# Turns for the rotating halves and a written order for VectorE in a dense expert pass

## The chip, the cores and the metric

The kernel runs on one core of one Trainium2 chip. The metric is the device time of one execution in microseconds; the kernel before takes 3657.54 us (median of three runs, 3656.35 to 3660.28). The engines are named as the profile names them: PE (TensorE, matrix products into PSUM), DVE (VectorE), ACT (ScalarE), POOL (GpSimd, which issues the gathers here) and SP (SyncE, which issues the other DMAs).

## The reference

One layer of a diffusion backbone for 9 tiles of 128 tokens (1 of context, 8 of latents): adaptive norm, one wide projection, a gated MLP over chunks, a bidirectional recurrent scan, a merge, and then PEER, a retrieval over 128 x 128 = 16384 single-neuron experts. The change lies in PEER, whose core is this:

```python
v1, i1 = lax.top_k(s[:, :, 0], PEER_TOPK)          # 8 heads, 16 of 128 keys, two halves
v2, i2 = lax.top_k(s[:, :, 1], PEER_TOPK)
cand = v1[..., :, None] + v2[..., None, :]         # 256 candidates a head
top_v, top_j = lax.top_k(cand, PEER_TOPK)          # 16 of them: expert numbers idx, gates g
...
ue = jnp.take(u_tab, ib, axis=0)                   # 128 experts a token
ve = jnp.take(v_tab, ib, axis=0)
a = jax.nn.gelu(jnp.einsum('bd,bed->be', xb, ue)) * gb
return jnp.einsum('be,bed->bd', a, ve)
```

Everything is in fp32 (the large products as three products of split halves).

## The kernel before

PEER is done in two ways. Four of the nine token tiles (GATHER) fetch the rows of their chosen experts: for each of 128 chosen experts of a token, POOL gathers a row of `u_tab` (tile `gu`), DVE takes its dot product with the token (`jk`, one instruction a row), after 16 rows ACT applies gelu (`act`), DVE multiplies by the gates, and then 16 rows of `v_tab` (`gv`) are added into `acc`, one DVE instruction each. A gathered tile has 256 such rows. The other five tiles (DENSE, 640 tokens) compute all 16384 experts with a gate matrix that is nearly empty: this is the dense pass, 128 expert tiles e of 128 experts.

For an expert tile, `hidden` makes 48 matmuls (two halves of 320 tokens, eight pieces of depth, three products of split halves) into PSUM tiles `pH`, ACT applies gelu into `a`, DVE multiplies by the gates `Gt`, and `a` is split into `aH` (ACT) and `aL` (DVE). Two 512 KB tables are loaded by SP and split in the same way: u (for the expert tile after) and v. The output product of three token tiles (`out_res`, 18 matmuls an expert tile) stays in six PSUM banks `pout` over the whole pass. For the other two token tiles there is no bank left: `out_rot` makes, after every GI = 4 expert tiles, four groups of 12 matmuls (two token tiles, two halves of 512 columns, the products of four expert tiles), each into a PSUM tile `prot`, which DVE adds into `accd` in SBUF. `pH` and `prot` share two PSUM banks (tag "tp", `ptp`); a new one must wait until the one two before has been read.

The gathered rows of three tiles are interleaved with this pass. `fill`, called behind each split and each addition, advances the gather by 1.525 rows on the average (6.1 an expert tile) and, when the tile before has fewer than 60 rows left, the rest of the routing of the next gathered tile (`combine_late`: its last top 16, the expert numbers `ix` and gates `ga`, in tiles `late`, `cmp`, `prod` on DVE), at 3 steps a call for the first and 0.8 for the others. Rows live in six buffers (tag "grow": four and two), in four while such a combine runs.

The order of the instructions on each engine is made by a scheduler from the program's order, the dependencies and its own estimate of times. `fill` and `paced` add a dependency without a wait: a row stands, in DVE's order, behind the split or addition that came KEEP = 2 before. Otherwise DVE's order is the scheduler's.

Before that, in the second half of the mixer, `build_G` makes the gates for the dense pass: for four tokens at a time, eight matmuls of 128 columns (`pG`, from one-hot tiles `oh` that DVE and ACT make) give the gates of four tokens, token by token in 512 columns of a PSUM tile of the same two banks, and two ACT instructions copy them into `Gs`, whose inner index is the token; `Gs` goes to HBM (`G_d`) and comes back in the dense pass as `Gt`.

Names in the order and the trace are those of the tiles; `oh`, `pG`, `Gs` belong to lines 523 to 558, the combine's DVE instructions to line 119, the rows to 802 to 820, the splits to 99 (ACT) and 100 (DVE), the additions to 1050 and 1052, the gate product to 1069, the three products of a matmul to 129 to 131.

Of the kernel before, what the change touches and what calls it, by code (L numbers as in the profile page):

```python
# [51 lines left out]
def hybrid_kernel(ctx, tc, x_all, pos, c2t, w_ada, b_ada, wst, wspt, bsp, lbraw, vecs, fng, skt, state,  # L52
# [56 lines left out]

    def paced(ins):  # L110
        if anchors:
            tc.add_manual_dep(ins.ins, anchors[0].ins.name,
                              mybir.DependencyInfo(mybir.DependencyClass.NoSync, mybir.DependencyReason.DATA),
                              reason="pace of the filling work")
# [400 lines left out]
    def build_G(gp, i, rt, rg, gl, tags):  # L515
# [22 lines left out]
        for t0 in range(0, 128 + 2 * OT, OT):  # L538
            if t0 < 128:
                ahead.append(one_hots(t0))  # L540
            if t0 >= 2 * OT:
                oh, og = ahead.popleft()
                tc0 = (t0 - 2 * OT) % TB
                if tc0 == 0:
                    tag = tags[(t0 - 2 * OT) // TB % len(tags)]
                    Gs = [gp.tile([128, 64, TB], F32, name="Gs", tag=tag, bufs=2) for _ in range(2)]
                pg = ptp("pG")
                for tt in range(OT):
                    for a in range(2):
                        P.matmul(pg[:, tt * 128:(tt + 1) * 128], oh[:, 0, :, tt], og[a][:, :, tt],  # L550
                                 start=(a == 0), stop=(a == 1))
                for z in range(2):
                    A.activation(Gs[z][:, :, tc0:tc0 + OT].rearrange("p i t -> p t i"),
                                 pg.rearrange("p (t i) -> p t i", t=OT)[:, :, z * 64:(z + 1) * 64],
                                 AF.Copy, scale=1.0 / 16384)
                if tc0 == TB - OT:
                    for z in range(2):
                        nc.sync.dma_start(G_d[i * (128 // TB) + (t0 - 2 * OT) // TB][:, z * 64:(z + 1) * 64, :],
                                          Gs[z])
            yield  # L560
# [452 lines left out]
    def fill(ins):  # L1013

        anchor(ins, KEEP)
        k = lates - len(late_q)
        if late_q and nrow[0] >= 256 * k - LEAD:
            owed[0] = owed.get(0, 0) + LATE[k > 0]
# [6 lines left out]
        advance(gather_q, RATE[4] * GI / (3 * GI + 2 * ROT))  # L1025

    def load_split(src, nm, bufs):
        raw = dp.tile([128, 1024], F32, name=nm + "r", tag="raw", bufs=3)
        nc.sync.dma_start(raw, src)
        H, L = [dp.tile([128, 1024], F32R, name=nm + z, bufs=bufs) for z in "HL"]  # L1030
        fill(split(raw, H, L))
# [9 lines left out]
    def out_rot(grp):  # L1041
        for i in range(ROT):
            t = slice((RES + i) * 128, (RES + i + 1) * 128)
            for n in range(2):
                s = slice(n * 512, n * 512 + 512)
                pr = ptp("prot")
                for m, (_, aH, aL, vH, vL) in enumerate(grp):
                    mmx(pr, [aH[:, t], aL[:, t]], [vH[:, s], vL[:, s]], m == 0, m == len(grp) - 1)
                if grp[0][0] == 0:
                    ins = V.tensor_copy(accd[i][:, s], pr)  # L1050
                else:
                    ins = V.tensor_tensor(out=accd[i][:, s], in0=accd[i][:, s], in1=pr, op=OP.add)  # L1052
                fill(ins)
    grp = []
    for e in range(129):
        if e < 128:
# [12 lines left out]
            V.tensor_tensor(out=ab, in0=ab, in1=Gt[:, :, e % GI, :], op=OP.mult)  # L1069
            aH, aL = [dp.tile([128, TD], F32R, name="a" + z, bufs=GI + 1) for z in "HL"]  # L1070
            fill(split(a, aH, aL))
            if 0 < e < 127:
                u = load_split(ut[e + 1], "u", 2)
            v = load_split(vt[e], "v", GI + 1)
        if e > 0:
            out_res(*grp[-1])
            if e % GI == 0:
                out_rot(grp)
                grp = []
# [114 lines left out]
```

## Time and profile before

| | us |
|---|---|
| median of three runs | 3657.54 |
| the profiled execution | 3668.42 |
| its span | 3666.6 |
| PE busy / DVE busy / ACT busy / POOL busy in the span | 3343.5 / 2841.6 / 1156.4 / 1436.9 |
| end of the gate build (last `Gs` copy starts) | 1736.1 |
| dense pass (first `pout` to the end of the last `prot`) | 1752 to 3644 |

The profile is of one execution. Its busy time of PE counts matmuls that overlap, so distances of starts tell more than durations; the granted clock is a share of PE's full 2.4 GHz, and a stretch that shows 0.93 had parts at half of it. A wait is shown with what ended it. The page's costliest groups of matmuls are those of `hidden` (L129 to L131, `pH`), of `out_res` (`pout`) and of `out_rot` (`prot`).

### The profile page before, as it was taken

The page shows a single profiled execution, that of the slowest core. Times are in us where ns is not written, and L with a number is a line of the kernel's source. Part 1 is how long each engine was busy: PE and PEld are TensorE (multiplying, and loading weights), DVE is VectorE, ACT ScalarE, POOL GpSimd, SP SyncE. Part 2 cuts the span into 40 slices and gives each one's busy share as a digit, 9 for nine tenths or more (in the row PEclk, how much of TensorE's full clock was granted, in tenths as well). Part 3 has the DMA queues.
Part 4 walks back from the last instruction along what each step waited for, and adds up shares of the span by engine and source line. Part 5 has one row for each costly group of instructions (what it writes and reads, how often), then busy time and mean ns, then how long its engine had stood idle before and what let it go on. Part 6 is the DMA issues. An engine that isn't in the chain of part 4 may idle for free. (4 is left out here: it accounts for less than half of the span.)

```text
span 3666.6 us, 48822 instructions
## 1 busy us (share of the span) xinstructions
PE 3343.5 (91%) x17547; PEld 2763.0 (75%) x17547; DVE 2841.6 (77%) x5427; ACT 1156.4 (32%) x2075; POOL 1436.9 (39%) x1128
## 2 busy tenths in 40 slices
PE   8888889898898899897899999989999989999997
PEld 4376778676576576576788888888898878898996
DVE  2317888787699986598787889887888888788888
ACT  2511334321323577726222222222222222222222
POOL 0002441454211220000265564655555456555654
PEclk9899999899999899897899999999999999999998
DMA  7787754688733676442898998898988799988986
GB/s 279 280 294 255 248 186 129 206 301 333 251 116 99 224 264 228 161 151 101 272 333 307 319 325 274 317 317 313 321 315 313 260 330 338 321 303 314 332 317 248
DMA packets 361956, 971.12 MB, mean 265 GB/s; under 512 B 32720, under 2 KB 142672, under 8 KB 356080
## 3 DMA queue, kind: packets, MB, share of 16 engines
q0 software_dynamic: 149824, 546.37, 42.3%
q1 hardware_dynamic: 211888, 421.62, 33.3%
q8 instruction: 138, 2.26, 0.2%
q14 instruction: 106, 0.87, 0.1%
HBM read 897.07 MB, written 70.80 MB: 264 GB/s over the span
## 5 line engine op out<-in xcount | busy, mean ns | idle before, releaser
L802 POOL DMA_INDIRECT gu<-in_urow_dram,ix x512 | 688.5, 1345 | 1003.7 <-DVE jk L805 374.1
L815 POOL DMA_INDIRECT gv<-in_vrow_dram,ix x512 | 694.9, 1357 | 736.4 <-DVE acc L820 399.9
L805 DVE SCALAR_TENSOR_TENSOR jk<-gu,h2r 128x1024 f16<-128x1024 f32 x512 | 625.6, 1222 | 139.9 <-DMA gu<-in_urow_dram,ix 124.8
L820 DVE SCALAR_TENSOR_TENSOR acc<-gv,act,acc 128x1024 f32<-128x1024 f32 x508 | 651.7, 1283 | 62.8 <-DMA gv<-in_vrow_dram,ix 53.3
L129 PE MATMUL pH<-h2DH,uH 128*128 128x320 f32 x2016 | 625.4, 310 | 12.9 <-DVE accd L1052 10.9
L131 PE MATMUL pH<-h2DH,uL 128*128 128x320 f32 x2016 | 622.9, 309 | 3.2 <-DVE uL L100 3.2
L130 PE MATMUL pH<-h2DL,uH 128*128 128x320 f32 x2016 | 623.4, 309 | 0.0
L129 PEld LDWEIGHTS pH<-h2DH,uH 128*128 128x128 f32 x2016 | 379.7, 188 | 23.0 <-DVE accd L1052 15.9
L130 PEld LDWEIGHTS pH<-h2DL,uH 128*128 128x128 f32 x2016 | 379.6, 188 | 4.4
L131 PEld LDWEIGHTS pH<-h2DH,uL 128*128 128x128 f32 x2016 | 379.4, 188 | 4.1 <-DVE uL L100 4.1
L129 PE MATMUL pout<-vH,aH 128*128 128x512 f32 x768 | 299.0, 394 | 23.0 <-ACT vH L99 16.3
L99 ACT ACTIVATE vH<-vr 128x1024 fp32r<-128x1024 f32 x128 | 133.4, 1058 | 568.9 <-DMA vr<-in_vrow_dram 294.3
L130 PE MATMUL pout<-vL,aH 128*128 128x512 f32 x768 | 302.0, 393 | 5.0 <-DVE vL L100 5.0
L131 PE MATMUL pout<-vH,aL 128*128 128x512 f32 x768 | 302.0, 393 | 2.1 <-DVE aL L100 2.1
L129 PE MATMUL prot<-vH,aH 128*128 128x512 f32 x512 | 211.7, 414 | 56.9 <-DVE accd L1052 50.8
L99 ACT ACTIVATE wH<-wraw 128x1024 fp32r<-128x1024 f32 x118 | 124.9, 1060 | 437.9 <-PE pq L130 145.2
L100 DVE TENSOR_TENSOR vL<-vr,vH 128x1024 fp32r<-128x1024 f32 x128 | 156.3, 1221 | 86.9 <-ACT vH L99 84.5
L130 PE MATMUL prot<-vL,aH 128*128 128x512 f32 x512 | 208.4, 407 | 0.0
L99 ACT ACTIVATE uH<-ur 128x1024 fp32r<-128x1024 f32 x126 | 133.3, 1058 | 237.1 <-PE pH L130 197.5
L131 PE MATMUL prot<-vH,aL 128*128 128x512 f32 x512 | 207.7, 406 | 0.0
L99 ACT ACTIVATE aH<-a 128x640 fp32r<-128x640 f32 x128 | 94.2, 736 | 357.1 <-DVE a L1069 284.2
L550 PEld LDWEIGHTS <-oh 128*128 128x128 f16 x1280 | 130.5, 120 | 80.7 <-issue 65.0
(343 smaller groups left out, 6442.7 us busy)
## 6 DMA issues: line engine op xcount, KB each, us to landing
wraw<-in_wst_dram SPq DMA_DIRECT2D x216, 512.0 KB
vr<-in_vrow_dram SPq DMA_DIRECT2D x128, 512.0 KB
ur<-in_ut_dram SPq DMA_DIRECT2D x126, 512.0 KB
G_d<-Gs SPq DMA_DIRECT2D x40, 1024.0 KB
Gt<-G_d SPq DMA_DIRECT2D x160, 256.0 KB
wraw<-in_w_ada_dram SPq DMA_DIRECT2D x48, 512.0 KB
gu<-in_urow_dram,ix POOLq DMA_INDIRECT x512
gv<-in_vrow_dram,ix POOLq DMA_INDIRECT x512
```

The source lines that it names most:

```text
L99: A.activation(H, src, AF.Copy)
L100: return V.tensor_tensor(out=L, in0=src, in1=H.bitcast(F32), op=OP.subtract)
L129: P.matmul(ps, a[0], b[0], start=first, stop=False)
L130: P.matmul(ps, a[0], b[1], start=False, stop=False)
L131: P.matmul(ps, a[1], b[0], start=False, stop=last)
L550: P.matmul(pg[:, tt * 128:(tt + 1) * 128], oh[:, 0, :, tt], og[a][:, :, tt], start=(a == 0), stop=(a == 1))
L802: G.indirect_dma_start(out=ur, out_offset=None, in_=urow, in_offset=bass.IndirectOffsetOnAxis(ap=ix[:, c:c + 1], axis=0))
L805: paced(V.scalar_tensor_tensor(jk, ur, 1.0, h2r, op0=OP.mult, op1=OP.mult, accum_out=dots[:, k:k + 1]))
L815: G.indirect_dma_start(out=vr, out_offset=None, in_=vrow, in_offset=bass.IndirectOffsetOnAxis(ap=ix[:, c:c + 1], axis=0))
L820: paced(V.scalar_tensor_tensor(acc, vr, act[:, k:k + 1], acc, op0=OP.mult, op1=OP.add))
```

## The change

Three things are changed. In the dense pass `out_rot` makes one of its four groups behind each expert tile, in turns, over the (up to) four expert tiles since its last turn; at the end all four are brought up to date. DVE's instructions of the pass (products with the gates, splits, additions, rows, the steps of the late combines) are chained in the order of the program by dependencies without a wait (`pin`), and the calls that advance rows and combines stand at five fixed places of a turn, with weights that add up to the rate of before; the split of u now stands ahead of that of a. In `build_G` the PSUM tile is laid out with the token innermost: matmuls write every fourth word, and ACT reads it in order.

```diff
--- before.py
+++ after.py
@@ -107,8 +107,21 @@
         while len(anchors) > keep:
             anchors.popleft()
 
+    pinned = []
+
+    def pin(ins):
+
+        if pinned[0] is not None:
+            tc.add_manual_dep(ins.ins, pinned[0].ins.name,
+                              mybir.DependencyInfo(mybir.DependencyClass.NoSync, mybir.DependencyReason.DATA),
+                              reason="order of the dense pass")
+        pinned[0] = ins
+        return ins
+
     def paced(ins):
-        if anchors:
+        if pinned:
+            pin(ins)
+        elif anchors:
             tc.add_manual_dep(ins.ins, anchors[0].ins.name,
                               mybir.DependencyInfo(mybir.DependencyClass.NoSync, mybir.DependencyReason.DATA),
                               reason="pace of the filling work")
@@ -544,14 +557,14 @@
                 if tc0 == 0:
                     tag = tags[(t0 - 2 * OT) // TB % len(tags)]
                     Gs = [gp.tile([128, 64, TB], F32, name="Gs", tag=tag, bufs=2) for _ in range(2)]
-                pg = ptp("pG")
+
+                pg = ptp("pG").rearrange("p (i t) -> p i t", t=OT)
                 for tt in range(OT):
                     for a in range(2):
-                        P.matmul(pg[:, tt * 128:(tt + 1) * 128], oh[:, 0, :, tt], og[a][:, :, tt],
+                        P.matmul(pg[:, :, tt], oh[:, 0, :, tt], og[a][:, :, tt],
                                  start=(a == 0), stop=(a == 1))
                 for z in range(2):
-                    A.activation(Gs[z][:, :, tc0:tc0 + OT].rearrange("p i t -> p t i"),
-                                 pg.rearrange("p (t i) -> p t i", t=OT)[:, :, z * 64:(z + 1) * 64],
+                    A.activation(Gs[z][:, :, tc0:tc0 + OT], pg[:, z * 64:(z + 1) * 64, :],
                                  AF.Copy, scale=1.0 / 16384)
                 if tc0 == TB - OT:
                     for z in range(2):
@@ -1010,25 +1023,27 @@
     nrow[0] = 0
     lates = len(late_q)
 
-    def fill(ins):
-
-        anchor(ins, KEEP)
+    def rows(n):
+
         k = lates - len(late_q)
         if late_q and nrow[0] >= 256 * k - LEAD:
-            owed[0] = owed.get(0, 0) + LATE[k > 0]
+            owed[0] = owed.get(0, 0) + LATE[k > 0] * n / 1.5
             while owed[0] >= 1 and lates - len(late_q) == k:
                 owed[0] -= 1
                 if next(late_q[0], 0) == 0:
                     late_q.popleft()
         busy = late_q and nrow[0] >= 256 * (lates - len(late_q)) - LEAD
         rows_of[:] = [(gat, NGR)] * NGR + [(dp, NGD)] * (0 if busy else NGD)
-        advance(gather_q, RATE[4] * GI / (3 * GI + 2 * ROT))
-
-    def load_split(src, nm, bufs):
+        advance(gather_q, n * RATE[4] / 6)
+
+    def load_raw(src, nm):
         raw = dp.tile([128, 1024], F32, name=nm + "r", tag="raw", bufs=3)
         nc.sync.dma_start(raw, src)
+        return raw
+
+    def parts(raw, nm, bufs):
         H, L = [dp.tile([128, 1024], F32R, name=nm + z, bufs=bufs) for z in "HL"]
-        fill(split(raw, H, L))
+        pin(split(raw, H, L))
         return H, L
 
     def out_res(e, aH, aL, vH, vL):
@@ -1038,19 +1053,22 @@
                 s = slice(n * 512, n * 512 + 512)
                 mmx(po[i][n], [aH[:, t], aL[:, t]], [vH[:, s], vL[:, s]], e == 0, e == 127)
 
-    def out_rot(grp):
-        for i in range(ROT):
-            t = slice((RES + i) * 128, (RES + i + 1) * 128)
-            for n in range(2):
-                s = slice(n * 512, n * 512 + 512)
-                pr = ptp("prot")
-                for m, (_, aH, aL, vH, vL) in enumerate(grp):
-                    mmx(pr, [aH[:, t], aL[:, t]], [vH[:, s], vL[:, s]], m == 0, m == len(grp) - 1)
-                if grp[0][0] == 0:
-                    ins = V.tensor_copy(accd[i][:, s], pr)
-                else:
-                    ins = V.tensor_tensor(out=accd[i][:, s], in0=accd[i][:, s], in1=pr, op=OP.add)
-                fill(ins)
+    def out_rot(z, grp, first):
+
+        i, n = divmod(z, 2)
+        t = slice((RES + i) * 128, (RES + i + 1) * 128)
+        s = slice(n * 512, n * 512 + 512)
+        pr = ptp("prot")
+        for m, (_, aH, aL, vH, vL) in enumerate(grp):
+            mmx(pr, [aH[:, t], aL[:, t]], [vH[:, s], vL[:, s]], m == 0, m == len(grp) - 1)
+        if first:
+            pin(V.tensor_copy(accd[i][:, s], pr))
+        else:
+            pin(V.tensor_tensor(out=accd[i][:, s], in0=accd[i][:, s], in1=pr, op=OP.add))
+    NZ = 2 * ROT
+    assert NZ == GI
+    done = [0] * NZ
+    pinned.append(None)
     grp = []
     for e in range(129):
         if e < 128:
@@ -1066,17 +1084,23 @@
                 a = dp.tile([128, TD], F32, name="a", bufs=2)
                 hidden(a, u)
             ab = a.rearrange("p (b t) -> p b t", t=TB)
-            V.tensor_tensor(out=ab, in0=ab, in1=Gt[:, :, e % GI, :], op=OP.mult)
+            pin(V.tensor_tensor(out=ab, in0=ab, in1=Gt[:, :, e % GI, :], op=OP.mult))
+            if 0 < e < 127:
+                u = parts(load_raw(ut[e + 1], "u"), "u", 2)
+            rows(1)
             aH, aL = [dp.tile([128, TD], F32R, name="a" + z, bufs=GI + 1) for z in "HL"]
-            fill(split(a, aH, aL))
-            if 0 < e < 127:
-                u = load_split(ut[e + 1], "u", 2)
-            v = load_split(vt[e], "v", GI + 1)
+            pin(split(a, aH, aL))
+            rows(1.5)
+            v = parts(load_raw(vt[e], "v"), "v", GI + 1)
+            rows(1.5)
         if e > 0:
             out_res(*grp[-1])
-            if e % GI == 0:
-                out_rot(grp)
-                grp = []
+            turns = [(e - 1) % NZ] if e < 128 else [(e - 1 + k) % NZ for k in range(NZ)]
+            for z in turns:
+                out_rot(z, [g for g in grp if g[0] >= done[z]], done[z] == 0)
+                done[z] = e
+            grp = grp[-(GI - 1):]
+        rows(2)
         if e < 128:
             grp.append((e, aH, aL, *v))
     gt2 = dp.tile([128, D], F32R, name="gt2d", tag="vH", bufs=GI + 1).bitcast(F32)
```

DVE, in the middle of the pass, where a group's addition stands (`a<-a,Gt` is the gate product, `uL`, `aL`, `vL` the splits, `jk` rows, `accd` the additions). Before, all four additions of four expert tiles:

```order
L100 TENSOR_TENSOR aL<-a,aH 128x640
L805 SCALAR_TENSOR_TENSOR jk,dots<-gu,h2r 128x1024 x2
L1052 TENSOR_TENSOR accd_13757<-accd_13757,prot 128x512
L805 SCALAR_TENSOR_TENSOR jk,dots<-gu,h2r 128x1024 x2
L1052 TENSOR_TENSOR accd_13757<-accd_13757,prot 128x512
L805 SCALAR_TENSOR_TENSOR jk,dots<-gu,h2r 128x1024 x2
L1052 TENSOR_TENSOR accd_13758<-accd_13758,prot 128x512
L805 SCALAR_TENSOR_TENSOR jk,dots<-gu,h2r 128x1024
L100 TENSOR_TENSOR vL<-vr,vH 128x1024
L1052 TENSOR_TENSOR accd_13758<-accd_13758,prot 128x512
L805 SCALAR_TENSOR_TENSOR jk,dots<-gu,h2r 128x1024
```

After, one turn and the product that begins the next:

```order
L1087 TENSOR_TENSOR a<-a,Gt 128x640
L100 TENSOR_TENSOR uL<-ur,uH 128x1024
L818 SCALAR_TENSOR_TENSOR jk,dots<-gu,h2r 128x1024
L100 TENSOR_TENSOR aL<-a,aH 128x640
L818 SCALAR_TENSOR_TENSOR jk,dots<-gu,h2r 128x1024 x2
L100 TENSOR_TENSOR vL<-vr,vH 128x1024
L818 SCALAR_TENSOR_TENSOR jk,dots<-gu,h2r 128x1024
L1067 TENSOR_TENSOR accd_13758<-accd_13758,prot 128x512
L818 SCALAR_TENSOR_TENSOR jk,dots<-gu,h2r 128x1024 x3
L1087 TENSOR_TENSOR a<-a,Gt 128x640
```

One addition stands in each turn, behind four rows, and the four additions in a row are gone.

DVE, at the start of the pass, around the split of u that the first `hidden` inside the pass needs (`a_13069` is the second expert tile). Before:

```order
L100 TENSOR_TENSOR aL<-a_13069,aH 128x640
L119 TENSOR_TENSOR cmp<-late,cs_13760 128x2048
L100 TENSOR_TENSOR uL<-ur,uH 128x1024
L119 TENSOR_TENSOR prod<-cmp,late 128x2048
L119 TENSOR_TENSOR late<-late 128x128
L119 TENSOR_TENSOR prod<-prod 128x8x128
L100 TENSOR_TENSOR vL<-vr,vH 128x1024
```

After:

```order
L132 TENSOR_REDUCE late<-late 128x8
L132 RECIPROCAL late<-late 128x8
L132 TENSOR_TENSOR late<-late 128x128
L132 COPY ga_13863<-late 128x128
L132 SCALAR_TENSOR_TENSOR ix_13865<-late 128x128
L818 SCALAR_TENSOR_TENSOR jk,dots<-gu,h2r 128x1024 x2
L1087 TENSOR_TENSOR a_13069<-a_13069,Gt 128x640
L100 TENSOR_TENSOR uL<-ur,uH 128x1024
```

The gate product of the second expert tile and the split of u have moved behind the end of the combine (`ix` holds the row numbers) and behind two gathered rows.

DVE, in the second late combine, with its casts (`CAST`) and the compare and multiply after them (`cmp`, `prod`). Before:

```order
L119 TENSOR_TENSOR late<-late 128x8x15
L805 SCALAR_TENSOR_TENSOR jk,dots<-gu,h2r 128x1024
L119 TENSOR_TENSOR cmp<-late,cs_13760 128x2048
L805 SCALAR_TENSOR_TENSOR jk,dots<-gu,h2r 128x1024
L1069 TENSOR_TENSOR a<-a,Gt 128x640
L119 MEMSET late 128x8
L100 TENSOR_TENSOR uL<-ur,uH 128x1024
L100 TENSOR_TENSOR aL<-a,aH 128x640
L805 SCALAR_TENSOR_TENSOR jk,dots<-gu,h2r 128x1024
L119 TENSOR_TENSOR prod<-cmp,late 128x2048
L100 TENSOR_TENSOR vL<-vr,vH 128x1024
```

After:

```order
L100 TENSOR_TENSOR vL<-vr,vH 128x1024
L132 CAST late<-late 128x256
L132 CAST late<-late 128x128
L132 TENSOR_TENSOR cmp<-late,cs_13760 128x2048
L132 TENSOR_TENSOR late<-late 128x8x15
L132 MEMSET late 128x8
L132 TENSOR_TENSOR prod<-cmp,late 128x2048
L818 SCALAR_TENSOR_TENSOR jk,dots<-gu,h2r 128x1024 x2
L1067 TENSOR_TENSOR accd_13757<-accd_13757,prot 128x512
```

Before, its instructions lie one by one between rows; now they stand as a block between the split of v and the addition.

## Rows read from the trace of the kernel before

**Rows 1.** Busy time, dense pass by stretch: start:end, length, engines (count), clock, DMA.

```profile
1752.00:1802.00 50.00, 45.30 (x240) 40.01 (x240) 41.00 (x118) 16.41 (x21) 9.67 (x10) 0.96 0.72 242
1802.00:2210.00 408.00, 387.32 (x2120) 350.55 (x2121) 338.35 (x414) 97.04 (x143) 238.10 (x177) 0.96 0.91 319
2210.00:2310.00 100.00, 88.61 (x463) 78.66 (x462) 89.30 (x185) 22.35 (x31) 50.02 (x37) 0.93 0.78 261
2310.00:2880.00 570.00, 547.93 (x3030) 493.86 (x3030) 467.19 (x568) 139.78 (x206) 325.34 (x238) 0.99 0.91 319
2880.00:2970.00 90.00, 77.12 (x390) 66.47 (x389) 77.06 (x165) 18.76 (x26) 44.19 (x34) 0.94 0.77 249
2970.00:3644.00 674.00, 658.77 (x3652) 596.88 (x3650) 566.39 (x678) 166.31 (x247) 388.29 (x285) 0.99 0.90 320
```

The engines' columns are PE, PEld (weight loads), DVE, ACT and POOL.

**Rows 2.** Timeline of PE: start, duration, instruction.

```profile
2603.68 0.40 PE L129 MATMUL pout<-vH,aH 128*128 128x512 f32 x1
...
2607.78 0.31 PE L129 MATMUL pH<-h2DH,uH 128*128 128x320 f32 x1
...
2614.82 0.40 PE L129 MATMUL pout<-vH,aH 128*128 128x512 f32 x1
```

**Rows 3.** Waits of PE in the pass: waiter, releaser, us in total, times, longest.

```profile
PE prot L129 <- DVE accd L1052: 50.8, 15, 9.3
...
PE pH L129 <- DVE accd L1052: 10.9, 4, 6.9
```

**Rows 4.** Timeline of ACT in the same turn.

```profile
2611.50 0.44 ACT L988 ACTIVATE a<-pH 128x320 f32<-128x320 f32 x1 [1.31 <-PE pH L131]
```

**Rows 5.** Timeline of DVE in and after that turn.

```profile
2613.74 5.24 DVE L820 SCALAR_TENSOR_TENSOR acc<-gv,act,acc 128x1024 f32<-128x1024 f32 x4
2618.90 1.22 DVE L100 TENSOR_TENSOR vL<-vr,vH 128x1024 fp32r<-128x1024 f32 x1
2620.04 0.82 DVE L1069 TENSOR_TENSOR a<-a,Gt 128x640 f32<-128x640 f32 x1
2620.77 1.22 DVE L100 TENSOR_TENSOR uL<-ur,uH 128x1024 fp32r<-128x1024 f32 x1
2621.91 0.82 DVE L100 TENSOR_TENSOR aL<-a,aH 128x640 fp32r<-128x640 f32 x1
...
2649.51 0.68 DVE L1052 TENSOR_TENSOR accd<-accd,prot 128x512 f32<-128x512 f32 x1
```

**Rows 6.** Waits of DVE for gathered rows in the pass.

```profile
DVE jk L805 <- DMA gu<-in_urow_dram,ix: 75.3, 34, 6.3
...
DVE acc L820 <- DMA gv<-in_vrow_dram,ix: 17.5, 15, 4.9
```

**Rows 7.** Timeline of DVE at the start of the pass.

```profile
1748.62 1.56 DVE L1069 TENSOR_TENSOR a<-a,Gt 128x640 f32<-128x640 f32 x2 [14.84 <-DMA Gt<-G_d]
...
1786.04 0.29 DVE L119 SCALAR_TENSOR_TENSOR ix<-late 128x128 int32<-128x128 f32 x1
1794.78 1.22 DVE L805 SCALAR_TENSOR_TENSOR jk<-gu,h2r 128x1024 f16<-128x1024 f32 x1 [8.45 <-issue]
```

**Rows 8.** Timeline of PE there.

```profile
1762.94 0.42 PE L131 MATMUL pH<-h2DH,uL 128*128 128x320 f32 x1 [1.73 <-DVE uL L100]
```

**Rows 9.** Busy time of line 119 alone: the stretch, DVE's busy time (count).

```profile
2210.00:2310.00 100.00, 23.42 (x102) 0.93 0.78 261
```

**Rows 10.** Tile Gs: operation, count, duration in ns (min/median/max), first and last start.

```profile
L553 ACT ACTIVATE Gs<-pG x320: 579/664/822, 1222.7 to 1736.1; 128x256 f32<-128x256 f32 x160
```

**Rows 11.** Busy time at the end of the gate build.

```profile
1710.00:1720.00 10.00, 7.07 (x57) 6.22 (x57) 8.28 (x19) 10.00 (x29) 0.00 (x0) 0.50 0.52 213
```

**Rows 12.** Busy time in the middle of the gate build.

```profile
1400.00:1500.00 100.00, 99.86 (x505) 63.65 (x504) 65.74 (x124) 70.09 (x174) 1.02 (x2) 1.00 0.54 204
```

**Rows 13.** Timeline of PE in that stretch.

```profile
1443.47 1.80 PE L550 MATMUL pG<-oh 128*128 128x128 f16 x16
1445.09 1.04 PE L127 MATMUL prow<-wraw,mg 128*128 128x512 f32 x2
```

## The prediction

> **What bounds the kernel now.** I read the page first, then the stretches of the dense pass, the waits of PE and DVE inside it, and single instructions of one turn. The dense pass runs from 1752 to 3644 us, half of the span. In its stretches [rows 1] the reader is to see PE busy for 1805 of 1892 us (the sum of the six) and a granted clock under 1.00 in each. One hidden matmul costs 7.04/48 = 0.147 us (2607.78 to 2614.82, 48 of them) and one output matmul 4.10/18 = 0.228 us (2603.68 to 2607.78, 18 of them) [rows 2]. The pass has 126 x 48 of the first and 128 x 30 of the second: 887 + 876 = 1763 us at the full clock. So it loses about 130 us: 87 us idle (1892 - 1805), and 43 us to the clock, taken as length times (1 - clock) [rows 1]. By stretch, idle plus clock: 6.7 us up to 1802, where the first late combine runs; 37.0; 18.4 around the second combine (2210 to 2310); 27.8; 18.3 around the third (2880 to 2970); 21.9. Sum 130; 87 of it lies in the three stretches without a combine. There PE waits for the additions into `accd`: 50.8 + 10.9 us of waits [rows 3], and I put the clock's share down to the same waits, since the stretches with the most idle time (11 and 14%) have the lowest clock (0.93 and 0.94 [rows 1]). The cause can be read from the code and the order: four rotating groups of 12 matmuls (2.7 us each) follow each other on two PSUM buffers, and each addition stands behind whatever DVE has in front of it, rows whose DMA may be late among them.
>
> **The change, part by part.** Work is neither added nor removed on PE: each expert still has 48 + 18 + 12 matmuls. DVE gets 131 additions for 128, 3 x 0.6 = 2 us, beside PE's work.
>
> *Steady turn.* After, one group of 12 comes per expert. Its buffer is the one that the second hidden half of the next expert needs. From the end of one second half to the start of the next PE has 18 + 12 output matmuls and 24 hidden ones: 6.84 + 3.52 = 10.36 us, whatever their order. In that time ACT and DVE must get through a fixed chain up to the addition. ACT's gelu starts 0.20 us after the first half's end (2607.78 + 24 x 0.147 = 2611.30, start 2611.50) and takes 0.44 [rows 4]. Then DVE, by distances of starts [rows 5]: gate product 0.73 (2620.04 to 2620.77), u split 1.14, a split 0.73 (as the product, the same shape), v split 1.14 (2618.90 to 2620.04), four rows 5.16 at most (2613.74 to 2618.90, in a run; apart, a little less), and the addition takes 0.68. Sum 0.64 + 0.73 + 1.14 + 0.73 + 1.14 + 5.16 + 0.68 = 10.22. It fits, by only 0.1 us, and some 0.3 with rows that stand apart. All but two of the turns in the new order have four rows ahead of the addition. Behind it stand two or three rows (2.5 to 3.8 us) and then DVE waits for the next gelu, about 2 us of a 13.9 us turn. So PE should not stop in an undisturbed turn. If the chain were 0.5 us longer than I take it, 0.2 us a turn over 115 turns would be 23 us lost; if shorter, nothing is gained, PE being full.
>
> What is left of the 87 us: 24 switches from dots to outputs, at which DVE needs an ACT result (in some of them ACT's order puts v's first half behind it, about 1 us late), estimated 7 us; three gather tiles that end, with the square of the sum standing in ACT's queue ahead of a gelu, about 3.5 us each, 11 us; late rows 5; clock 3. Sum 26, a gain of 61. Late rows are the weak figure. Before, DVE waited 75.3 + 17.5 us for rows in 49 waits [rows 6]. Below, none (six buffers, and a row's buffer is needed again only a turn later); above, the share that stands ahead of the addition, 4 of 6.1 rows: 61 us in 32 waits, less 0.3 us of slack each, 51 us. I take 5, nearer to the lower end: the first row of all came 8.5 us after its index (written by 1786.3, row at 1794.8, DVE idle for 8.45 us [rows 7]), and the new order leaves nearly 13.9 us.
>
> *Start of the pass.* Here the fixed order costs. Before, the u split that hidden tile 2 needs stood amid the combine, and the matmul that waited for it ran at 1762.94 [rows 8]. After, DVE does the product of expert 0 (1748.62 [rows 7]), the whole first combine (23.42 us busy for one that lies wholly in a stretch [rows 9]) with the splits of a and v, 2 us more, and then two gathered rows, whose gathers can only start when the combine has made their indices. Only behind them stand the product of expert 1 and the u split. The combine ends near 1775, the rows come 8.5 us later and take 2.5 us, the u split ends near 1788.5. PE's matmul that waits for it moves from 1763 to 1788.5, 25.5 us; about 1 us of other work is done earlier, and I add 3 us for a clock at its lower level (1.2 GHz) when PE resumes, an estimate. Cost 27 us. It could be 15, if the combine alone in front of DVE runs faster and the rows come in half the time, or 35.
>
> *Second and third combine.* Their 23.4 us of DVE work [rows 9] now stand at counted places inside four turns, partly ahead of the addition. For the second: turn one holds 1.1 + 1.7 + 1.7 us there, turn two 1.7 + 4.2, turn three 3.0 + 3.45; less the slack 4, 5.5 and 6 us. In two of these turns DVE also waits for ACT results that ACT makes only after the next gelu: about 2.5 and 5.5 us. Sum 24, with the clock 29, in place of 18.4. The third has less ahead of the addition: 19, with the clock 23, in place of 18.3. DVE's 2 us of idle time in four turns could hide 8 us of such a block at most, so 15 is the lower bound, and 40 the upper, if the combine's input comes late as well.
>
> *PSUM layout of the gate build.* The pG matmuls now write every fourth word, and ACT reads 256 contiguous words and writes runs of four. The Gs copy takes 664 ns at the median [rows 10]; a contiguous ACT read of 320 words takes 0.44 us [rows 4]. So a copy becomes between 0 and 0.22 us shorter. At the end of the build (1688 to 1737) ACT is busy without a gap (10.00 of 10) and DVE 8.28 [rows 11]; 57 matmuls in 10 us make a period of 2.8 us for 16. ACT would save up to 0.8 us in each of 16 periods, DVE limits that to 17%, 0.5 us: 8 us at most. I take 7. For the first four tiles PE is busy all the time where the build is densest, 99.86 of 100 us [rows 12], so ACT's gain is hidden there, and 1024 matmuls that became slower would show. No row shows a matmul with a strided output; I take no loss and bound it below at nothing and above at the rival's upper end.
>
> The Trainium skill, "PSUM — Partial Sum Buffer" (Specifications), speaks against this part: PSUM lines are 8 bytes, and it says that any non-contiguous pattern slows matmuls significantly. By it the sum would take the second rival's price; no run here has shown such a write.
>
> *Moved loads.* SP issues ur and vr in the same alternation; a raw buffer is needed three loads later, over a turn. The gates' loads come four turns ahead. I cost both at nothing. The end of the pass has the same last steps (rmsnorm and store of five tiles) behind the last matmuls, so also nothing.
>
> **Sum.** Pass: 26 + (6.7 + 27) + 29 + 23 = 112 in place of 130, gain 18. Build: 7. Together 25 us. The profiled execution took 3668.4 us (span 3666.6), 10.9 above the median of 3657.5: 3643 there, 3632 as median.
>
> **Rivals.** (1) *Rows come late ahead of the addition*: the place is the four rows between gate product and addition; the price 51 us from above, against 5: 3632 + 46 = 3678, slower. It decides once more than 26 of the 46 us come true. For it: 93 us of row waits [rows 6]. Against it: they fell where DVE ran rows in runs of five; an even pace asks for a row every 2.3 us. (2) *Strided matmuls slow down*: between 320 and 512 columns a column costs (0.228 - 0.147)/192 = 0.42 ns and a matmul 12 ns beside, so 128 columns 66 ns; doubled, 120. The build's matmuls now come 0.10 us apart (16 of them from 1443.47 to 1445.09 [rows 13]), so 1024 x 19 ns = 19 us, and the time 3651, no change; at four times a column's price, 227 ns, it is 128 us and 3760. For it nothing in the trace, against it nothing either. This is the case that the skill's sentence makes. (3) *The combines cost no more than before*: start 13 us cheaper, windows at 18 each, 28 us: 3604. For it: DVE has idle time beside them; against it, the fixed places.
>
> **How the numbers follow.** Forecast 0.50 (its own range 3610 to 3655), rival 1 0.18, rival 2 0.12, rival 3 0.20. The range reaches from rival 3 past its point, 3595, to rival 1, 3680; the upper end of rival 2 is left out. What can be told from no change is 0.2%, 7 us: faster under 3650. Faster: 0.45 + 0.20 = 0.65. Same: 0.05 of the forecast, 0.05 of rival 1 and 0.07 of rival 2, 0.17. Slower 0.18.
>
> **What would show it.** Right: waits of prot and pH for `accd` nearly gone outside three places, PE over 99% busy in between and clock 1.00; PE idle some 25 us from 1761 on, with DVE waiting for the first gathered row; PE stops of 4 to 6 us in the turns that hold a combine; the end of the build 7 us shorter with Gs under 0.5 us. Wrong: a pH wait for `accd` of a few tenths in each turn (the chain is longer than the sum), row waits between product and addition, pG matmuls further apart than before, or a start without the gap.

## The result and the profile after

The changed kernel takes 3830.45 us (median of 4 runs, 3829.41 to 3838.04), the kernel before 3656.94 us beside it: a ratio of 1.0477, 95% interval 1.0462 to 1.0492. The forecast was 3632 us, and the time lies far outside its range.

The stretches of the dense pass after, cut as in [rows 1] (first the start with the first combine, then in turn the stretches without and with a combine):

```profile
1736.00:1786.00 50.00, 19.38 (x60) 15.78 (x61) 40.26 (x112) 8.60 (x10) 15.81 (x13) 0.62 0.55 188
1786.00:2270.00 484.00, 445.08 (x2399) 394.42 (x2397) 360.47 (x435) 110.63 (x161) 251.19 (x185) 0.98 0.85 291
2270.00:2370.00 100.00, 78.89 (x416) 69.89 (x416) 88.08 (x180) 20.98 (x30) 44.98 (x33) 0.95 0.71 238
2370.00:2960.00 590.00, 547.21 (x2943) 486.33 (x2942) 450.85 (x571) 137.05 (x199) 311.91 (x231) 0.98 0.87 299
2960.00:3070.00 110.00, 86.23 (x430) 76.76 (x429) 88.52 (x161) 23.22 (x32) 48.96 (x37) 0.88 0.69 237
3070.00:3807.00 737.00, 679.92 (x3648) 605.35 (x3646) 556.26 (x671) 167.40 (x245) 376.63 (x280) 0.97 0.84 288
```

The pass lasts 2071 us in place of 1892. Idle time of PE plus length times (1 - clock), as in the prediction, is 49.6 us at the start, 26.1 and 37.0 us around the two later combines, and 48.6 + 54.6 + 79.2 = 182 us in the three stretches between, where [rows 1] give 87 and the forecast had 26. Most of the loss is there. DVE, ACT, POOL and the DMA engines are all less busy there than before: nothing is full, everything waits.

What PE waits for in the pass, answering [rows 3] (waiter, releaser, us, times, longest):

```profile
PE pH L142 <- ACT a L1001: 99.9, 63, 6.9
PE pout L143 <- DVE vL L100: 57.9, 45, 7.7
PE pout L142 <- ACT aH L99: 47.0, 7, 21.0
...
PE prot L142 <- DVE accd L1067: 0.2, 1, 0.2
```

The additions into `accd` are waited for no more, as forecast. In their place stand the Gelu and v's split. One engine further on, the waits of ACT and of DVE:

```profile
ACT vH L99 <- DMA vr<-in_vrow_dram: 617.6, 120, 11.9
ACT uH L99 <- DMA ur<-in_ut_dram: 584.4, 103, 11.7
...
DVE a L1087 <- ACT a L1001: 408.5, 115, 12.5
```

The same waits in the kernel before, which the prediction had not looked at:

```profile
ACT vH L99 <- DMA vr<-in_vrow_dram: 294.3, 71, 8.5
...
ACT uH L99 <- DMA ur<-in_ut_dram: 16.1, 6, 6.0
...
DVE a L1069 <- ACT a L988: 8.4, 5, 3.1
```

Here is the chain of the work that ended last after the change, followed through one turn of the steady part and into the next (start, us, what; "issue" is time in which the engine waited for nothing that the profile shows, here an engine's own distance between instructions):

```profile
2644.92 9.56 DMA ur<-in_ut_dram
...
2662.31 1.23 DVE vL L100
2663.60 6.51 DMA ur<-in_ut_dram
2670.17 0.04 issue
2670.21 1.06 ACT uH L99
2671.27 0.33 ACT a L1001
2671.67 0.70 issue
2672.37 0.92 DVE uL L100
2673.29 0.21 issue
2673.51 1.28 DVE acc L833
2674.79 0.07 DVE aL L100
2674.86 0.58 issue
2675.44 1.29 DVE acc L833
2676.78 1.17 issue
2677.95 1.23 DVE vL L100
2679.24 4.40 DMA ur<-in_ut_dram
```

The reader is to see a ring. It starts at v's split and is back there 15.64 us later (2662.31 to 2677.95), where PE's own turn (one expert tile at the full clock) is 13.9 us. Rounds differ with their load: the one before took 18.61 us (2643.70 to 2662.31, with the load of 9.56 us), the one after 13.54. PE does not stand in this round at all. Its links are: v's split, held at its fixed place late in the turn, gives the raw buffer free (three buffers, u and v in turn); u's load goes out at once and lands 6.5 us later; ACT makes u's high half; the second Gelu of the turn, behind it in ACT's queue, runs; DVE's product waits for that Gelu, and behind the product stand, in the program's order, u's split, a row, a's split, rows, and v's split. ACT's queue in this part of the program reads (the number is the place on the engine, the names' numbers tell the tiles apart):

```
1416 L1001 ACTIVATE a_21953<-pH_21954 128x320
1417 L99 ACTIVATE uH_22135<-ur_22133 128x1024
1418 L1001 ACTIVATE a_21953<-pH_21980 128x320
1419 L99 ACTIVATE aH_22017<-a_21953 128x640
1420 L99 ACTIVATE vH_22159<-vr_22157 128x1024
```

`uH_22135` belongs to the expert two ahead; no one needs it before the next turn. The scheduler puts it between the two Gelus of expert `a_21953`. It did the same in most turns of the kernel before, where it cost little (16.1 us of waits for u's loads): there DVE made its halves close behind ACT's, the buffers came free early, and a u load went out 19.1 us ahead of its use (median over 126 loads, from issue to the start of its `uH`). After, it is 6.7 us.

### The profile page after: what moved, and what is told of

It is laid out like the page before. It is cut to its first block, busy times and chain, and to the rows that moved or that the text cites. A ratio compares the mean times of both kernels' runs of the same rounds, so it can differ in the third digit from the quotient of the medians.

```text
span 3829.5 us, 48883 instructions
## 1 busy us (share of the span) xinstructions
PE 3398.9 (89%) x17547; PEld 2793.6 (73%) x17547; DVE 2843.8 (74%) x5430; ACT 1110.8 (29%) x2075; POOL 1427.4 (37%) x1128
## 4 chain that ended last, share of the span: by engine, by line
DMA 21%; DVE 15%; PE 9%; issue 8%; ACT 5%; POOL 2%; SPq 0%; ACTq 0%; POOLq 0%; DVEq 0%
DMA ur<-in_ut_dram 16%; DMA vr<-in_vrow_dram 3%; DVE jk L818 3%; DVE acc L833 3%; DVE uL L100 3%; ACT uH L99 3%; DVE vL L100 2%; PE pH L142 1%; PE pH L143 1%; DMA gv<-in_vrow_dram,ix 1%; PE pH L144 1%; DVE late L132 1%; ACT a L1001 1%; POOL gu L815 1%; POOL gv L828 1%
## 5 line engine op out<-in xcount | busy, mean ns | idle before, releaser
L828 POOL DMA_INDIRECT gv<-in_vrow_dram,ix x512 | 679.5, 1327 | 867.3 <-DVE acc L833 511.6
L142 PE MATMUL pH<-h2DH,uH 128*128 128x320 f32 x2016 | 655.1, 325 | 100.3 <-ACT a L1001 99.9
L144 PE MATMUL pH<-h2DH,uL 128*128 128x320 f32 x2016 | 643.7, 319 | 8.1 <-DVE uL L100 8.1
L143 PE MATMUL pH<-h2DL,uH 128*128 128x320 f32 x2016 | 643.0, 319 | 0.0
L142 PEld LDWEIGHTS pH<-h2DH,uH 128*128 128x128 f32 x2016 | 397.4, 197 | 146.4 <-ACT a L1001 139.9
L1087 DVE TENSOR_TENSOR a<-a,Gt 128x640 f32<-128x640 f32 x128 | 105.6, 825 | 427.3 <-ACT a L1001 408.5
L144 PEld LDWEIGHTS pH<-h2DH,uL 128*128 128x128 f32 x2016 | 397.4, 197 | 11.6 <-DVE uL L100 10.7
L143 PEld LDWEIGHTS pH<-h2DL,uH 128*128 128x128 f32 x2016 | 397.5, 197 | 6.0
L143 PEld LDWEIGHTS pout<-vL,aH 128*128 128x128 f32 x768 | 145.1, 189 | 99.0 <-DVE vL L100 77.7
L142 PEld LDWEIGHTS pout<-vH,aH 128*128 128x128 f32 x768 | 144.8, 189 | 85.8 <-ACT aH L99 49.1
```

The costliest lines, as they stand in the source:

```text
L142: P.matmul(ps, a[0], b[0], start=first, stop=False)
L143: P.matmul(ps, a[0], b[1], start=False, stop=False)
L144: P.matmul(ps, a[1], b[0], start=False, stop=last)
L828: G.indirect_dma_start(out=vr, out_offset=None, in_=vrow, in_offset=bass.IndirectOffsetOnAxis(ap=ix[:, c:c + 1], axis=0))
L1087: pin(V.tensor_tensor(out=ab, in0=ab, in1=Gt[:, :, e % GI, :], op=OP.mult))
```

## Experiments

Each was timed beside the kernel before; the ratio is to that. Theory A is the ring above.

**1. ScalarE's order alone.** u's high half goes behind the copy aH:

```
+                if e > 1:
+                    after(highs[-1], aHs[-1])   # uH behind aH on ScalarE
```

(`after` adds a dependency without a wait; lines that only keep the two instructions at hand are left out.)

> The changed kernel with one thing else: on ScalarE the high half of the u split of the expert two ahead stands behind the copy aH of the turn, not between the two Gelus of the turn. Theory A (a loop once a turn: VectorE's half of the v split, held at its fixed place, frees the raw buffer; only then is the next u load issued; it lands 6.7 us later; its high half stands in ScalarE's order ahead of the second Gelu; the gate product and so all of VectorE's fixed order wait for that Gelu): the loop is opened, the waits of the gate product for the Gelu fall from 408 us to under 150 us, TensorE's waits for Gelu and for vL in the pass from 158 us to under 50 us, and the time to 3640 to 3690 us. Theory B (the 16 DMA engines, 80 to 90% busy in the pass, give the raw loads too little): as many bytes in the same order, 3800 to 3840 us. Theory C (a rotating half every turn takes one of the two PSUM banks of the hidden tiles, so that the next hidden half waits for the second Gelu): 3780 to 3830 us, and the waits of pH for the Gelu stay near 100 us.

3672.44 us, ratio 1.0040 (1.0024 to 1.0055): inside A's span, 158 us back from one dependency a turn on ScalarE. What is left of ACT's wait for u's loads and of PE's for the Gelu:

```profile
ACT uH L106 <- DMA ur<-in_ut_dram: 96.7, 27, 9.6
...
PE pH L149 <- ACT a L1008: 26.3, 9, 5.8
```

The DMA engines carry more here, not less (0.93 busy from 3070 to 3570, after the change 0.85): theory B falls, and C with it, since the PSUM banks are as they were. DVE's wait for the Gelu, forecast under 150 us, still is 233.5 us.

**2. The pins off u's and v's split.**

```
-        pin(split(raw, H, L))
+        split(raw, H, L)
```

> The changed kernel without the pins on the u and v splits alone (rows, gate product, a's split and additions stay pinned in the program's order); the scheduler then puts the VectorE halves of u and v a turn earlier, close behind ScalarE's halves. Theory A: raw buffers come free a turn earlier, u's load is issued 15 us and more ahead of its use, the loop is open: 3640 to 3690 us. Theories B and C: the loads' bytes and the PSUM banks are as they were, 3780 to 3840 us.

3633.09 us, ratio 0.9937 (0.9922 to 0.9952). This is the time that was forecast for the change (3632 us), but in part by errors that cancel, in a kernel with other pins. Idle time plus clock, in stretches cut as before, is 47.5 us at the start (forecast 33.7), 23.2 and 21.7 us around the two combines (29 and 23) and 11.9 us between (26). The u loads go out 20.6 us ahead (median). PE's longest waits in the pass:

```profile
PE pout L142 <- ACT aH L99: 27.8, 3, 26.1
PE pH L142 <- DVE accd L1067: 23.9, 5, 7.3
```

and the engines' busy time from 3070 to 3570 us, in the columns of [rows 1]:

```profile
3070.00:3570.00 500.00, 500.00 (x2790) 450.97 (x2790) 421.47 (x517) 131.62 (x186) 296.21 (x219) 1.00 0.93 326
```

PE is busy for 500.00 of 500 us at clock 1.00; before, it was 486.72 in the same stretch, and in the changed kernel 455.01.

**3. Other buffers.** `tag="raw", bufs=3` became two for u and one for v.

> The changed kernel with the three raw buffers divided: two for u alone, one for v alone. A u load is then freed by u's own split, nearly a turn and a half ahead of its use; a v load is issued behind the v split of the turn before. ScalarE's order, which is not pinned, then has the v half between the two Gelus. Theory A: the loop stays, with v's load in the place of u's: 3770 to 3840 us, and ScalarE waits for vr rather than ur. Theory D (three buffers are simply too few for loads that must be ahead; any kind that gets a turn more of lead helps, whatever ScalarE's order): 3650 to 3720 us. Theory B: 3800 to 3840 us, both kinds of waits as now.

3898.93 us, ratio 1.0652 (1.0636 to 1.0669), slower than the change itself. u's loads now lead by 12.2 us, and it doesn't help: v's load, behind the v split of the turn before, has taken their place, and the scheduler puts v's half between the Gelus. ACT's wait for it:

```profile
ACT vH L99 <- DMA vr<-in_vrow_dram: 842.5, 127, 14.4
```

So it isn't that u had too few buffers (D falls), but that some load closes the ring. A's sign was right, its size was not (3770 to 3840).

**4. The same buffers, with both halves behind aH** (the edit of 1, for v too).

> The changed kernel with the raw buffers divided (two for u, one for v, as in the run that was 7% slower than before) and the high halves of both u and v behind the turn's copy aH on ScalarE. All pins on VectorE stay, and the v load is still issued only behind the v split of the turn before. Theory A (only a load whose high half stands ahead of the second Gelu closes the loop): both are out of it, 3625 to 3675 us, ScalarE's waits for the loads under 400 us where the divided buffers alone had 842 us for vr, and no PE wait for Gelu or vL over 30 us. Theory F (splits pinned at the end of the turn free the buffers too late, whatever ScalarE's order; the run with the u half moved was lucky in its buffers): 3750 us or more.

3691.52 us, ratio 1.0098 (1.0077 to 1.0119): 207 us less than 3 by ScalarE's order alone, though 16 us over A's span. vH waits 103.8 us for its loads. F falls.

**5. Rows behind v's split.** The two `rows(1.5)` around v's split became one `rows(3)` behind it.

> The changed kernel with one thing else: the one or two rows that stand between a's split and v's split on VectorE stand behind v's split, with the rows that are there already. As many rows and the same instructions in a turn. Theory A (the loop from the v split over u's load, ScalarE and the second Gelu back to the v split): it becomes shorter by 1.5 rows of 1.25 us, 1.9 us a turn, about what a turn has over its nominal length (the pass's 2070 us less 1760 us of matmul pitch, less 33 us at the start and some 45 us at the two later combines, over 128 turns: 1.8 us): 3640 to 3700 us. Theory E (VectorE's fixed order is too long by itself, wherever the rows stand in the turn): 3815 to 3845 us.

3755.61 us, ratio 1.0261 (1.0217 to 1.0306): 75 us back, half of what A said, and E falls too. PE's wait for vL shrank to 5.1 us, but that for the Gelu stayed at 103.9. The chain of the work that ended last shows why, here one round of it in this kernel:

```profile
3106.64 1.15 DVE uL L100
3107.85 7.32 DMA vr<-in_vrow_dram
3115.25 1.06 ACT vH L99
3116.30 0.34 ACT a L1001
3116.68 0.63 PE pH L142
...
3122.30 1.06 ACT uH L99
3123.36 0.33 ACT a L1001
3123.75 0.70 issue
3124.45 1.23 DVE uL L100
```

There is a second ring, which contains no rows: u's split frees v's load; v's half stands ahead of the first Gelu; the second hidden half on PE waits for that Gelu, the second Gelu for it (with u's half in front of it), and then product and u's split. This round is 17.8 us long (3106.64 to 3124.45), 7.32 of it the load. PE, which had stood idle, makes the first 15 of its 24 matmuls at half clock: they start 0.27 us apart, the others 0.147.

**6 and 7. v's half alone behind aH**, in the kernel of 5 and in the changed kernel.

> The kernel with the rows behind v's split (3756 us), with the high half of v behind the turn's copy aH on ScalarE, where it stood ahead of the first Gelu. Theory A2 (there are two loops: one from v's split over u's load and the second Gelu, one from u's split over v's load, v's high half, the first Gelu, the second hidden half on TensorE and the second Gelu back to u's split; moving the rows shortened only the first): the second is opened and TensorE's waits of pH for the Gelu (103.9 us) go under 40 us, 3640 to 3700 us. If the first loop, by its own length of some 13.5 us with loads of 7.5 us, still bound that kernel: 3735 to 3760 us.

3706.22 us, ratio 1.0113 (1.0092 to 1.0134): 49 us back, and pH's wait for the Gelu falls from 103.9 to 23.0 us, as expected of the second ring; 6 us short of the span, since pH now waits 82.0 us for uL.

> The changed kernel with the high half of v alone behind aH on ScalarE; u's high half stays ahead of the second Gelu and the rows stay ahead of v's split. Theory A2: the first loop, 15 us and more, is left as it was: 3780 to 3835 us, ScalarE's waits for ur stay over 500 us. If the loop over v's load is what sets most turns: under 3750 us.

3832.94 us, ratio 1.0467 (1.0419 to 1.0516), as the change. ACT's waits for ur are 694.4 us. With the second ring cut and the first left, nothing is gained: the first sets the turn.

**8. Turns without pins** (the kernel before with the new layout, and turns).

> The kernel before with the new layout of the gate build and the turns, and no pins: rows, combines and splits are filled in by the scheduler as before. If the turns are what takes the waits away and the pins only cost: 55 to 75 us less than the layout's run of 3655 us, 3580 to 3600 us, with no wait of 20 us at the start of the pass. If the pins are needed for the additions to be in time: 3640 to 3660 us.

3657.90 us, ratio 0.9997 (0.9979 to 1.0015): turns alone give nothing. The wait has only changed its name against [rows 3], in PE's waits:

```profile
PE pH L129 <- DVE accd L1051: 67.4, 25, 5.0
...
PE prot L129 <- DVE accd L1051: 5.4, 3, 4.2
```

The next hidden tile needs the addition's PSUM bank, and the addition still stands behind whatever rows the scheduler put in front of it. In sum 72.8 us, against 61.7 before.

**9. Pins without turns** (the kernel of 2 with the burst behind every fourth expert; unlike in the kernel before, no rows stand between the four additions).

> The kernel of the run with unpinned u and v splits, with the rotating halves not taking turns: all four in one burst behind every fourth expert, as before the change. What the turns are worth by themselves. If the waits of prot for the additions (75 us of TensorE's time in the kernel before) are due to the burst: 50 to 80 us more than that run's 3633 us, 3680 to 3715 us. If it was the scheduler's placing of rows ahead of the additions that made them late: 0 to 15 us more, 3630 to 3650 us.

3784.33 us, ratio 1.0350 (1.0304 to 1.0395), 151 us over the kernel of 2 and over both spans. With this order fixed, DVE can do nothing while it waits for the next of four groups, and what stands behind is late. A fixed order with rows between the additions was not run. The 75 us that the expectation gives for the kernel before are 61.7 by [rows 3], with the waits of pH. The wait of DVE, of this kernel's waits:

```profile
DVE accd L1067 <- PE prot L144: 116.9, 31, 5.0
```

and the longest of PE:

```profile
PE prot L142 <- DVE accd L1067: 90.1, 27, 6.8
```

**10. The layout alone** (the kernel before with the gate build of the change).

> The kernel before with the gate build's layout alone (matmuls that write every fourth column of the PSUM tile, copies that read it straight). From the profile after, where the first output matmul comes at 1736.4 us instead of 1752.0 us and a copy takes 379 ns instead of 664 ns: 10 to 18 us faster, 3639 to 3647 us, ratio 0.995 to 0.997. The other reading (the build ended earlier in the changed kernel because of the order of VectorE that the pass begins with, not because of the layout): within 3 us of before.

3655.42 us beside 3658.84, ratio 0.9980 (0.9967 to 0.9994): 2 to 12 us. The interval reaches into the spans of both readings, so it shows a gain and not which reading is right. The copies of the build, by tile as in [rows 10]:

```profile
L554 ACT ACTIVATE Gs<-pG x320: 356/379/417, 1222.3 to 1731.2; 128x256 f32<-128x256 f32 x160
```

and its matmuls:

```profile
L551 PE MATMUL pG<-oh x1280: 269/302/502, 1219.7 to 1730.5; 128*128 128x128 f16 x183
```

A copy is 285 ns shorter than in [rows 10]. From the first pG matmul to the last it is 510.8 us, before 515.0 (1220.3 to 1735.3), after the whole change 508.8 (1211.5 to 1720.3). So some 9 of the 15.6 us by which the pass begins earlier after the change lie ahead of the build, in code that the change leaves alone; over the kernels with the new layout the first pG matmul came anywhere from 1211.5 to 1219.7 us. Why is open.

**11. Combines spread thinner** in the kernel of 2: `LATE = (3, 0.8)` became `(1, 0.4)`, and the rate of the rows 6.2 for 6.1.

> The kernel with unpinned u and v splits, with the pieces of the late combines spread: one piece in 1.5 row places for the first combine (three before) and 0.4 for the later ones (0.8 before), and the rows at 6.2 for 6.1, so that they end in the same turn. If the wait of 26 us at the start of the pass and the some 32 us at the two later combines are due to the density of their pieces in VectorE's fixed order: 25 to 40 us less than 3633 us, 3592 to 3610 us. If they are due to the combine's length as such (rows wait for it and are late): 3625 to 3640 us.

3633.85 us, ratio 0.9942 (0.9915 to 0.9969): nothing. The wait of 26 us at the start is gone, but the pass is as long as before (1864.0 us, in the kernel of 2 1863.5): the time came back in small pieces, among them 11.5 us in which PE waits for a's low half (1.5 us in the kernel of 2).

**12. No rows beside a late combine.**

```
-        advance(gather_q, n * RATE[4] / 6)
+        if not busy:
+            advance(gather_q, n * RATE[4] / 6)   # RATE[4] 6.1 -> 6.55, LATE (1, 0.8)
```

> The kernel with unpinned u and v splits, with no rows in the turns in which a late combine runs, 6.55 for 6.1 rows a turn in the others (as many rows in all, ending a turn earlier), and the first combine at one piece in 1.5 row places. If the waits around the combines are VectorE's work (a full turn has 12.4 us of it in 13.9 us, and a combine brings some 37 us, so that spreading the pieces among full turns only moved the waits): the two later combines go from some 32 us of waits to under 15 us and the start from 26 us to some 12 us, 3595 to 3615 us. If the higher rate of rows makes its own waits (6.55 rows are 12.9 us of VectorE a turn, and the DMA engines are at 0.94 in this kernel): 3630 to 3660 us.

3570.52 us, ratio 0.9762 (0.9746 to 0.9779), below its span and the lowest time of all. The 37 us of the expectation were too much ([rows 9]: 23.4 us), and it counted idle time alone, without the clock. The reading holds: what a combine brings must be taken from the rows of its own turns. The pass takes 1810 us of 1763 nominal, 53 less than in the kernel of 2; 7.6 us more come from a pass that begins earlier (1735.9 for 1743.5 us); why it does is open. Its first 50 us, in which PE was busy for 20.48 us at a clock of 0.64 in the kernel of 2, and a steady stretch, which PE fills:

```profile
1743.00:1793.00 50.00, 40.63 (x213) 35.59 (x212) 40.48 (x96) 13.52 (x18) 11.29 (x9) 0.94 0.56 178
...
2400.00:2800.00 400.00, 400.00 (x2235) 360.71 (x2235) 355.41 (x432) 104.30 (x149) 257.96 (x186) 1.00 0.97 345
```

## Why the prediction was wrong

**The step that failed** is the last of the change's parts, the moved loads: "a raw buffer is needed three loads later, over a turn ... I cost both at nothing." The three loads are right, the rest is not. Between the release of the buffer and the use of the load lies a full turn by the program, but ACT's queue takes the load's high half a whole turn before DVE needs it, ahead of a Gelu on which DVE's whole fixed order hangs. The cost was not 0 but about 160 to 200 us: 158 us by run 1, which moves nothing but that half, and 197 us by run 2, which gives the buffers back early and lets u's split move in DVE's order as well. The prediction listed what each pin put in front of DVE's instructions and never asked what a late DVE half holds: a buffer, and so a transfer.

**The steady chain** of 10.22 us in 10.36 rested on a Gelu that starts 0.20 us after the hidden half's end [rows 4]. In the changed kernel that start is set by u's load: the half of 2664.16 to 2667.68 had its Gelu at 2671.18, 3.5 us after. Where u's half no longer stands in front, the chain fits as worked out. In run 1, which keeps every pin, one turn takes 9.34 us from the product to the end of the addition (3297.62 to 3306.96; 9.58 by the sum), and PE is busy for 495.70 us of the 500 from 3070 at clock 1.00.

**Right:** the additions' waits, and a gap at the start, 21.0 us in place of 25.5, with DVE waiting for the first row. The 0.2 us left of the additions' waits are no test, since the ring holds PE up elsewhere; without it they come to 17.2 us in run 1 and 29.3 in run 2, against 61.7 [rows 3]. The row at the start:

```profile
1769.93 1.22 DVE L818 SCALAR_TENSOR_TENSOR jk<-gu,h2r 128x1024 f16<-128x1024 f32 x1 [5.26 <-DMA gu<-in_urow_dram,ix]
```

DVE stands idle for 5.26 us for it, where 8.45 us were taken from before [rows 7]. The start's idle time plus clock is 49.6 us against the 33.7 forecast (6.7 + 27): PE's clock is at 0.62 of full over it, and the 3 us put down for the clock were far too few. The second combine was 26.1 us for 29; the third 37.0 for 23, in a stretch that holds ring turns as well.

**The build** was put at 7 us; run 10 gives 2 to 12. The copy became 285 ns shorter, more than the 220 that the prediction allowed at most: it had set the time of 320 contiguous words against that of 256. From the first pG matmul to the last the build lost 4.2 us in run 10 and 6.2 after the whole change, under the 8 us that DVE was to allow; that DVE is what limits it is not shown.

**Rival 1** (late rows) did not come: DVE waited 22.3 + 11.3 us for rows in the pass, 92.8 before, and in run 1, where the turns are not drawn out by the ring, 21.9 + 10.2. **Rival 2** is there in small: in the layout's run 16 pG matmuls take 1.79 us to the next start,

```profile
1445.93 1.96 PE L551 MATMUL pG<-oh 128*128 128x128 f16 x16
1447.72 1.04 PE L127 MATMUL prow<-wraw,mg 128*128 128x512 f32 x2
```

0.112 us each in place of 0.101 [rows 13]: 11 ns more, where the rival was priced at 19. The Trainium skill, "PSUM — Partial Sum Buffer" (Specifications), which says that a non-contiguous pattern slows matmuls significantly, has the direction right, with 11 ns of 101; the net of the layout is a gain all the same. **Rival 3** did not come: it gave the start and the combines 21, 18 and 18 us, and they cost 49.6, 26.1 and 37.0. Spreading the combines gave nothing back (run 11), taking rows away did (run 12).

The chances had no case for a raw load: they went by DVE's time, late rows and strided matmuls. The profile's rows on ACT's waits for loads (294.3 us before), read beside the order of ACT and the new order of DVE, pointed to where the ring could close.

## What to carry to other kernels

When the order of one engine is fixed, follow each of its instructions to the buffer that it gives back, the transfer that waits for the buffer, and the in-order queue in which the transfer's first user stands; if that leads back to the engine, add up the ring and compare it with the turn. A ring showed here as a pass in which no engine is full, and in the chain of waits as the same few pieces again and again, with a DMA of several us in each round. Fix the order of the instructions that must be in time, and leave those that give buffers back free to run early.

## What the runs showed that was not expected

- Turns alone, pins with a burst of four additions, and pins with turns, each with the new layout and with u's and v's splits unpinned: 0.9997, 1.0350 and 0.9937 of the time before.
- Moving one ACT instruction of 1.06 us past one of 0.42 us and one of 0.74 us changed the time by 158 us.
- A raw load of 512 KB between other traffic lands 4.4 to 9.6 us after its issue in the same part of the pass; a ring with a load in it inherits that spread each turn.
- A strided pG matmul starts 11 ns later than a contiguous one, and the copy that reads it straight takes 379 ns in place of 664 ns.
